# Table loads ahead, dots two steps later, half of the score sums on GpSimd: four edits to the indexer stage of a hybrid attention layer

## The chip, the cores and the metric

The kernel runs on one core of one Trainium2 chip. The time is device microseconds of one launch, the median of three runs: 1025.65 us (1023.9 to 1025.77). Five engines work side by side, each through its own instructions in the order of the program: PE (TensorE: matmuls into PSUM), DVE (VectorE), ACT (ScalarE), POOL (GpSimd, which also issues some DMAs) and SP (SyncE, which issues most DMAs). An instruction that waits for another engine holds up everything behind it on its own engine.

## What is computed

One layer: a projection of 272 tokens (16 meta tokens and 256 of the sequence), sparse attention beside a pooling mixer, a norm, and a gated feed-forward part. The change touches the indexer, which says which keys each query may see. Cut to what matters (T is 272, 16 indexer heads of width 64, top 64 of the keys):

```python
p = h @ W_in            # q | c_kv | q_idx | k_idx | w_idx | u
c_kv = rms_norm(c_kv, kv_norm_g)
dots  = einsum('bqhd,bsd->bqhs', q_idx * 64**-0.5, k_idx)
score = einsum('bqhs,bqh->bqs', relu(dots), w_idx * 16**-0.5)
score = where(causal, score, NEG_INF)
_, sel = top_k(score, 64)
bias = rel_bias[t5_bucket(max(dist, 0))]     # one table of 32 buckets x 8 heads
logits = q_abs . c_kv[sel] * 128**-0.5 + bias
p = softmax(logits); out = p . c_kv[sel]
```

After that come the values, the pooling, W_o, two layer norms and the feed-forward part, which hold most of the time and are not touched.

## The kernel before

**Number format.** Nearly every float32 matrix is split into an upper and a lower part of a narrower format: ACT copies (the upper part), DVE subtracts (the lower part). For weights this is `split_part`, L193 on ACT and L194 on DVE. A product is then two or three matmuls for each of its 16 K steps of 128 rows. In the indexer's projections (`paired`) a step is two matmuls: L316 with 416 columns (upper weights with both parts of x) and L317 with 208 (lower weights with the upper part of x).

**Weight stream.** `stream` lists the weight tiles in order: tiles 0 to 7 are the indexer's query projections (w_proj), 8 and 9 are w_uk and w_uv, then the other w_proj tiles and all the rest. Each is 1 MB: a DMA on SP (L199) into one of three `wraw` buffers, then split by L193 and L194 in two halves of 1024 (tile 10 in pieces of 512 and 1536) into one of three `whl` buffers. `weights()` calls for the tile two ahead of the one used. The next load into a `wraw` buffer waits until L194 is through with the tile in it.

**Start.** x comes with the first weights (L334), ACT and DVE split both (L339 to L342), and PE projects the indexer's key, its head weights and the latent c_kv (L388). From PSUM ACT and DVE make `kidx` (L395, L397), `wt` (L400), `kt` (L415) and the squares (L418). PE turns `wt` (L423), DVE copies it to `widx` (L424), the 16 head weights of each query.

**Indexer stage.** The loop L489 runs over j = 0 to 7; iteration j projects the queries of heads 2j and 2j + 1 (a pair). At its end ACT takes one half of the sum from PSUM (L502, `whole`), DVE adds the other (L503), and both write the pair's query in two parts, `qi` (L506 on ACT, L508 on DVE). The dots of pair j - 1 stand within iteration j: `dots` for the first head after nine K steps, for the second after twelve. A head has four matmuls (L477, L478: 144 keys for the first block of queries, 272 for the second); ACT applies the relu into `rl` (L480 for the first block, L481 for the second); DVE adds it, times the head's weight, to `score` (L483, for each block). The latent norm hangs on the same loop: PE sums the squares (L363) after j = 0, DVE transposes (L368) and scales (L432), POOL takes the power -0.5 (L433), DVE spreads it (L372) and scales the latent (L439), ACT and DVE split it (L441, L442).

`relative_bias()` is called after j = 1: it loads the table of biases (`rb_sb`, L454) and the one-hot buckets (`oh`, L456), multiplies them (L458), writes the product behind a stretch of NEG into `strip` (L460, L461), sends it to DRAM (L463, a DMA on POOL) and reads it back as Toeplitz blocks (L468, three DMAs on POOL).

**Keys.** The loop L518 makes eight heads of keys from w_uk (L522 to L524, copied by L526 on ACT); the dots of the last pair stand after head h = 2, and after heads 1 and 3 w_uv is split. Then come the values (L554 to L559), the top-k on DVE (L575, L576), which masks the bias (L580), and the query projections. The bias is first used by L622.

**What sets the order.** The program is written as one list; a scheduler then orders each engine's instructions by their place in that list and by when it reckons that each may run, and gives out the buffers of a tag. Tiles of tag t (`temp`, four buffers: `wt`, `sq`, `r`, `rb`, `rl`, `whole`, `strip` and, before, the two tables) and of tag w (`window`, three buffers, used by the pooling later on) are such.

## Time and profile before

| what | value |
|---|---|
| median of three runs | 1025.65 us |
| the profiled execution, its own time | 1026.09 us |
| its span, first to last instruction | 1024.3 us |
| mean granted clock of TensorE | 0.994 |

The span by stages, from the windows of the trace (us; busy time of each engine):

| stretch | what runs | length | PE | DVE | ACT | POOL | clock |
|---|---|---|---|---|---|---|---|
| 0 to 24 | start | 24.00 | 22.03 | 15.34 | 16.55 | 3.55 | 1.00 |
| 24 to 49.8 | indexer, j = 0 to 2 | 25.80 | 21.43 | 19.42 | 14.12 | 7.74 | 0.87 |
| 49.8 to 83.4 | indexer, j = 3 to 7 | 33.60 | 30.34 | 25.46 | 21.20 | 0.03 | 1.00 |
| 83.4 to 98.7 | keys, last dots, values | 15.30 | 14.59 | 12.88 | 11.96 | 0.30 | 1.00 |
| 98.7 to 143.3 | queries, top-k | 44.60 | 44.60 | 29.96 | 19.24 | 0.00 | 1.00 |
| 143.3 to 968 | attention, pooling, W_o, feed-forward | 824.70 | 824.70 | 749.66 | 502.98 | 167.42 | 1.00 |
| 968 to 1024.3 | last part and norm | 56.30 | 50.77 | 39.54 | 36.31 | 11.64 | 0.94 |

How to read it: busy time is the time in which an engine ran an instruction, waits left out. A wait in the trace's lists stands as "engine line <- whom it waited for". In a row of the timeline the first two numbers are start and length in us, then engine, line, operation, what is written and read, shape, and in brackets the idle time before it and what ended it. In a row of the windows the stretch and its length come first, then busy time and instructions of PE, PE's weight load, DVE, ACT and POOL, then the granted clock, the share of the DMA engines and GB/s.

### The profile page before, as it was taken

The numbers are of one execution on the slowest core, as the hardware profiler recorded it, in microseconds if no ns is written. First come the engines' busy times: TensorE is split into PE (matmuls) and PEld (weight loads), VectorE is DVE, ScalarE is ACT, GpSimd is POOL, SyncE is SP. The second block draws the span as 40 slices with busy tenths as digits, with TensorE's granted clock in tenths as the row PEclk, the third lists the DMA queues.
The fourth block names the chain that finished last, engine by engine and source line by source line (L and its number), as shares of the span: only waits on it lengthen the run. The fifth ranks groups of instructions, "written<-read, shape, count | busy, mean of one in ns | idle before, by whom it ended". The sixth has DMA issues, their size and how long they took to land.

```text
span 1024.3 us, 18956 instructions
## 1 busy us (share of the span) xinstructions
PE 1008.5 (98%) x7516; PEld 958.8 (94%) x7516; DVE 892.2 (87%) x1409; ACT 622.4 (61%) x1008; POOL 190.7 (19%) x246
## 2 busy tenths in 40 slices
PE   9899999999999999999999999999999999999997
PEld 8788999999999999999999999999999999999986
DVE  6788768767879998899999999999999999999876
ACT  7567446655457765666556665666656666566674
POOL 1300004324430032203121021210212102120031
PEclk9899999999999999999999999999999999999998
DMA  9656543454653569999888888888888889888584
GB/s 330 224 194 228 192 154 130 145 170 164 207 202 134 196 190 264 284 367 304 274 282 288 297 281 272 281 290 291 284 274 286 285 292 283 273 284 288 209 250 131
DMA packets 59753, 250.26 MB, mean 244 GB/s; under 512 B 21734, under 2 KB 22416, under 8 KB 32656
## 3 DMA queue, kind: packets, MB, share of 16 engines
q1 hardware_dynamic: 34592, 230.42, 62.6%
q0 software_dynamic: 7888, 16.14, 8.3%
q10 hardware_dynamic: 17184, 2.49, 1.5%
q8 instruction: 59, 0.97, 0.4%
q14 instruction: 30, 0.25, 0.1%
HBM read 232.50 MB, written 2.11 MB: 229 GB/s over the span
## 4 chain that ended last, share of the span: by engine, by line
PE 90%; DVE 3%; DMA 3%; issue 2%; ACT 1%; POOL 1%; SPq 0%; POOLq 0%; ACTq 0%; DVEq 0%
PE mm L308 66%; PE at L920 6%; PE at L919 6%; PE at L921 6%; DVE whl L194 1%; PE mm L316 1%; ACT whl L193 1%; DMA wraw<-in_w_proj 1%; PE mm L317 1%; DMA wraw<-in_w_down 1%; DMA oh<-in_onehot 1%; DMA wraw<-in_w_first 1%; PE at L477 0%; PE mm L620 0%; PE at L478 0%
## 5 line engine op out<-in xcount | busy, mean ns | idle before, releaser
L308 PEld LDWEIGHTS mm<-hp,whl 128*128 128x128 f32 x3840 | 456.9, 188 | 6.3
L308 PE MATMUL mm<-hp,whl 128*128 128x258 f32 x3840 | 458.9, 279 | 0.0
L194 DVE TENSOR_TENSOR whl<-wraw,whl 128x1024 fp32r<-128x1024 f32 (+2 forms) x312 | 370.6, 1215 | 34.3 <-ACT whl L193 33.3
L193 ACT ACTIVATE whl<-wraw 128x1024 fp32r<-128x1024 f32 (+2 forms) x312 | 304.1, 1021 | 72.4 <-PE mm L308 23.5
L194 DVE TENSOR_TENSOR whl<-room,whl 128x512 fp32r<-128x512 f32 (+1 forms) x104 | 118.0, 1164 | 1.9 <-ACT whl L193 1.6
L193 ACT ACTIVATE whl<-room 128x512 fp32r<-128x512 f32 (+1 forms) x104 | 98.4, 993 | 14.9 <-DVE room L205 7.5
L308 PE MATMUL mm<-xp,whl 128*128 128x258 f32 (+4 forms) x768 | 98.8, 285 | 0.0
L308 PEld LDWEIGHTS mm<-xp,whl 128*128 128x128 f32 x768 | 93.8, 188 | 0.9
L850 ACT ACTIVATE z<-mm,cv 128x256 f32<-128x256 f32 x40 | 22.6, 564 | 89.3 <-PE mm L308 89.3
L892 POOL TENSOR_TENSOR forms<-za 128x128 f32<-128x128 f32 x20 | 20.3, 1016 | 295.2 <-DVE za L868 230.4
L850 ACT ACTIVATE za<-mm,cv 128x256 f32<-128x256 f32 x40 | 22.6, 564 | 84.9 <-PE mm L308 83.6
L920 PE MATMUL at<-whl,gp 128*128 128x512 f32 x180 | 70.6, 393 | 0.0
L921 PE MATMUL at<-whl,gp 128*128 128x512 f32 x180 | 70.4, 392 | 0.0
L919 PE MATMUL at<-whl,gp 128*128 128x512 f32 x180 | 68.7, 392 | 0.0
L895 POOL TENSOR_TENSOR forms<-za 128x128 f32<-128x128 f32 x20 | 22.5, 1124 | 196.7 <-DVE za L868 144.0
L308 PE MATMUL mm<-mixp,whl 128*128 128x258 f32 x384 | 48.0, 280 | 0.0
L308 PE MATMUL mm<-mixa,whl 128*128 128x258 f32 x384 | 47.1, 278 | 0.0
L308 PEld LDWEIGHTS mm<-mixp,whl 128*128 128x128 f32 x384 | 46.1, 188 | 0.1
L308 PE MATMUL mm<-fold,whl 128*128 128x260 f32 x384 | 45.8, 280 | 0.0
L308 PEld LDWEIGHTS mm<-mixa,whl 128*128 128x128 f32 x384 | 45.6, 188 | 0.0
L308 PEld LDWEIGHTS mm<-fold,whl 128*128 128x128 f32 x384 | 45.5, 188 | 0.1
L316 PE MATMUL mm<-xp,whl 128*128 128x416 f32 x128 | 41.7, 381 | 0.0
(342 smaller groups left out, 1470.4 us busy)
## 6 DMA issues: line engine op xcount, KB each, us to landing
wraw<-in_w_up SPq DMA_DIRECT2D x62, 1024.0 KB, 5.1
wraw<-in_w_down SPq DMA_DIRECT2D x54, 1024.0 KB, 6.7
room<-in_w_up SPq DMA_DIRECT2D x26, 1024.0 KB, 5.2
room<-in_w_down SPq DMA_DIRECT2D x26, 1024.0 KB, 6.5
wraw<-in_w_proj SPq DMA_DIRECT2D x24, 1024.0 KB, 5.0
wraw<-in_w_o SPq DMA_DIRECT2D x16, 1024.0 KB, 4.9
y<-v POOLq DMA_DIRECT2D x27, 256.0 KB, 8.4
y<-u POOLq DMA_DIRECT2D x18, 256.0 KB, 4.8
```

What stands on the lines that cost most here:

```text
L193: upper = nc.scalar.activation(hl[:, 0, c], raw[:, c], AF.Copy)
L194: lower = nc.vector.tensor_tensor(hl[:, 1, c], raw[:, c], hl[:, 0, c].bitcast(F32), op=ALU.subtract)
L308: nc.tensor.matmul(ps, a, b, start=n == 0 and i == 0, stop=i == 2 and n == KT - 1)
L316: nc.tensor.matmul(ps[:, :2 * m], hl[:, 0, w], act[k].both(lo, hi), start=n == 0, stop=False)
L317: nc.tensor.matmul(ps[:, m:2 * m], hl[:, 1, w], act[k][:, 0, lo:hi], start=False, stop=n == KT - 1)
L850: nc.scalar.activation(z, src[:, 2:NQ], AF.Identity, bias=col(C_B, j), scale=col(C_W, 3 * j + 2))
L892: nc.gpsimd.tensor_tensor(s[:, 0], a21, a22, op=ALU.add)
L895: nc.gpsimd.tensor_tensor(s[:, 3], a11, a21, op=ALU.subtract)
L919: nc.tensor.matmul(ps, a[:, 0, i], hl[:, 0, w], start=j == 0, stop=False)
L920: nc.tensor.matmul(ps, a[:, 0, i], hl[:, 1, w], start=False, stop=False)
L921: nc.tensor.matmul(ps, a[:, 1, i], hl[:, 0, w], start=False, stop=j == n - 1)
```

## The change

Four edits, all around the indexer stage:

- `rb_sb` and `oh` get tiles of tag w, and their loads are issued where the bias tiles are made, ahead of the stage. `whole` moves from tag t to tag w.
- The dots of a pair stand after 11 and 14 K steps, where they stood after 9 and 12.
- The score sum of the first block, one DVE instruction, becomes two on POOL: rl times the head's weight, in place, and score plus that.
- The dots of the last pair stand after key head 4, where they stood after head 2.

```diff
--- before.py
+++ after.py
@@ -449,11 +449,12 @@
 
         return bias[:, h, ::-1]
 
+    rb_sb = window("rb_sb")[:32, :H]
+    nc.sync.dma_start(rb_sb, rel_bias)
+    oh = window("oh")[:32, :T]
+    nc.sync.dma_start(oh, onehot)
+
     def relative_bias():
-        rb_sb = temp([32, H], "rb_sb")
-        nc.sync.dma_start(rb_sb, rel_bias)
-        oh = temp([32, T], "oh")
-        nc.sync.dma_start(oh, onehot)
         ps = small()
         nc.tensor.matmul(ps[:H, :T], rb_sb, oh, start=True, stop=True)
         strip = temp([H, STRIP], "strip")
@@ -479,9 +480,10 @@
             rl = temp([P, KW], "rl")
             nc.scalar.activation(rl[:, :KA], pa_[:, S * i:S * i + KA], AF.Relu)
             nc.scalar.activation(rl[:, KA:], pb[:, :T], AF.Relu)
-            for i2, (a, b) in enumerate(((0, KA), (KA, KW))):
-                nc.vector.scalar_tensor_tensor(score[:, a:b], rl[:, a:b], widx[:, i2, h:h + 1], score[:, a:b],
-                                               op0=ALU.mult, op1=ALU.add)
+            nc.vector.scalar_tensor_tensor(score[:, KA:], rl[:, KA:], widx[:, 1, h:h + 1], score[:, KA:], op0=ALU.mult,
+                                           op1=ALU.add)
+            nc.gpsimd.tensor_tensor(rl[:, :KA], rl[:, :KA], widx[:, 0, h:h + 1].to_broadcast([P, KA]), op=ALU.mult)
+            nc.gpsimd.tensor_tensor(score[:, :KA], score[:, :KA], rl[:, :KA], op=ALU.add)
 
     queries = sb.tile([P, 2, 2, S], F32R, name="qi", tag="y", padded_shape=[P, 2, 2, KT * T // 4])
     nc.gpsimd.memset(queries[:, :, :, :ALL].bitcast(F32), 0.0)
@@ -489,16 +491,16 @@
     for j in range(8):
         hl = weights()
         ps = big()
-        paired(ps, hl, x_parts, TOPK, T, K_PROJ, k1=9)
+        paired(ps, hl, x_parts, TOPK, T, K_PROJ, k1=11)
         if j:
             pa_ = small()
             dots(j - 1, qis[j - 1], pa_, (0,))
-        paired(ps, hl, x_parts, TOPK, T, K_PROJ, k0=9, k1=12)
+        paired(ps, hl, x_parts, TOPK, T, K_PROJ, k0=11, k1=14)
         if j:
             dots(j - 1, qis[j - 1], pa_, (1,))
-        paired(ps, hl, x_parts, TOPK, T, K_PROJ, k0=12)
+        paired(ps, hl, x_parts, TOPK, T, K_PROJ, k0=14)
         qi = queries[:, j % 2]
-        whole = temp([P, NI], "whole")
+        whole = window("whole")[:, :NI]
         nc.scalar.activation(whole, ps[:, NI:2 * NI], AF.Copy)
         nc.vector.tensor_tensor(whole, ps[:, :NI], whole, op=ALU.add)
         for i in range(2):
@@ -524,7 +526,7 @@
             nc.tensor.matmul(ps[:, :T], uk[:, 1, w], ctp[:, c, 0, :], start=False, stop=c == 1)
         with tc.issue_after(query):
             key = nc.scalar.activation(kt[:, h, :], ps[:, :T], AF.Copy)
-        if h == 2:
+        if h == 4:
             dots(7, qis[7], big(), (0, 1), big)
         if h in (1, 3):
```

The line numbers of the changed kernel run up to two higher in this stage (L477 is L478 there, L483 stays for the second block, L485 and L486 are the sums on POOL, L458 is L459, L502 is L504, L508 is L510).

Where instructions stand, in three places. First SP, at the start of the weight stream; `wraw` with a number is a buffer's tile. Before:

```order
L199 DMA wraw_387<-in_w_proj 128x2048
L199 DMA wraw_394<-in_w_proj 128x2048
L199 DMA wraw_401<-in_w_proj 128x2048
L199 DMA wraw_455<-in_w_proj 128x2048
L199 DMA wraw_545<-in_w_proj 128x2048
L199 DMA wraw_613<-in_w_proj 128x2048
L199 DMA wraw_681<-in_w_proj 128x2048
L454 DMA rb_sb_531<-in_rel_bias 32x8
L456 DMA oh_533<-in_onehot 32x272
L199 DMA wraw_749<-in_w_proj 128x2048
```

The changed kernel, from the same place:

```order
L453 DMA rb_sb_385<-in_rel_bias 32x8
L455 DMA oh_387<-in_onehot 32x272
L199 DMA wraw_391<-in_w_proj 128x2048
L199 DMA wraw_398<-in_w_proj 128x2048
L199 DMA wraw_405<-in_w_proj 128x2048
L199 DMA wraw_459<-in_w_proj 128x2048
L199 DMA wraw_547<-in_w_proj 128x2048
L199 DMA wraw_617<-in_w_proj 128x2048
L199 DMA wraw_687<-in_w_proj 128x2048
L199 DMA wraw_757<-in_w_proj 128x2048
```

The two small loads, which stood behind seven w_proj loads, now stand ahead of the first. The rows of x's load and of the later weights keep their places.

Second ACT, from the last instruction of the start to the end of iteration j = 0; `whl_388` is tile 0, 395 tile 1, 402 tile 2, 456 tile 3. Before:

```order
L340 ACTIVATE whl_169<-wraw_l_186 128x336
L193 ACTIVATE whl_388<-wraw_387 128x1024 x2
L395 ACTIVATE kidx_351<-mm_204 64x272 x2
L415 ACTIVATE kt_367<-mm_205 128x272
L415 ACTIVATE kt_367<-mm_206 128x272
L193 ACTIVATE whl_395<-wraw_394 128x1024 x2
L418 ACTIVATE sq_369<-mm_205 128x272
L418 ACTIVATE sq_373<-mm_206 128x272
L193 ACTIVATE whl_402<-wraw_401 128x1024 x2
L502 ACTIVATE whole_441<-mm_408 128x208
L193 ACTIVATE whl_456<-wraw_455 128x1024
L506 ACTIVATE qi_385<-whole_441 64x208 x2
```

The changed kernel, whose tiles 0 to 3 are 392, 399, 406 and 460:

```order
L340 ACTIVATE whl_169<-wraw_l_186 128x336
L193 ACTIVATE whl_392<-wraw_391 128x1024
L395 ACTIVATE kidx_351<-mm_204 64x272 x2
L415 ACTIVATE kt_367<-mm_205 128x272
L415 ACTIVATE kt_367<-mm_206 128x272
L193 ACTIVATE whl_392<-wraw_391 128x1024
L418 ACTIVATE sq_369<-mm_205 128x272
L418 ACTIVATE sq_373<-mm_206 128x272
L193 ACTIVATE whl_399<-wraw_398 128x1024 x2
L193 ACTIVATE whl_406<-wraw_405 128x1024 x2
L504 ACTIVATE whole_445<-mm_412 128x208
L193 ACTIVATE whl_460<-wraw_459 128x1024
```

The second half of tile 0 stood ahead of `kidx` and `kt` and now stands behind them. DVE has the same move: its L194 for that half stood ahead of L397 and L400 and now stands behind both, and both halves of tiles 1 and 2 follow it ahead of `whole`.

Third DVE in iterations j = 1 and 2, from the scaling of the latent norm (L432) to the second pair's query; `whl` is tile 3 first, then tile 4. Before:

```order
L432 TENSOR_SCALAR rms_v_382<-r_448 128x9
L194 TENSOR_TENSOR whl_456<-wraw_455,whl_456 128x1024
L483 SCALAR_TENSOR_TENSOR score_359<-rl_487,widx_376,score_359 128x144
L483 SCALAR_TENSOR_TENSOR score_359<-rl_487,widx_376,score_359 128x272
L483 SCALAR_TENSOR_TENSOR score_359<-rl_503,widx_376,score_359 128x144
L483 SCALAR_TENSOR_TENSOR score_359<-rl_503,widx_376,score_359 128x272
L372 STREAM_TRANSPOSE rb_523<-rms_v_382 128x288
L503 TENSOR_TENSOR whole_516<-mm_462,whole_516 128x208
L439 SCALAR_TENSOR_TENSOR kt_367<-kt_367,cv_193,rb_523 128x272 x2
L194 TENSOR_TENSOR whl_546<-wraw_545,whl_546 128x1024
L508 TENSOR_TENSOR qi_385<-whole_516,qi_385 64x208 x2
```

The changed kernel:

```order
L432 TENSOR_SCALAR rms_v_382<-r_452 128x9
L194 TENSOR_TENSOR whl_460<-wraw_459,whl_460 128x1024
L483 SCALAR_TENSOR_TENSOR score_359<-rl_495,widx_376,score_359 128x272
L372 STREAM_TRANSPOSE rb_529<-rms_v_382 128x288
L461 MEMSET strip_539 8x400
L483 SCALAR_TENSOR_TENSOR score_359<-rl_512,widx_376,score_359 128x272
L439 SCALAR_TENSOR_TENSOR kt_367<-kt_367,cv_193,rb_529 128x272 x2
L505 TENSOR_TENSOR whole_522<-mm_466,whole_522 128x208
L462 COPY strip_539<-at_537 8x272
L194 TENSOR_TENSOR whl_548<-wraw_547,whl_548 128x1024
L510 TENSOR_TENSOR qi_389<-whole_522,qi_389 64x208 x2
```

The two sums of 128x144 are gone; the memset of `strip` and its copy from PSUM (L461 and L462, before L460 and L461) now stand ahead of tile 4's first half and of the second pair's query, and `whole` stands behind the two L439. On POOL the sums of the first two heads stand between the power L433 and the DMA of `strip`, and those of the next two behind the three DMAs that read it back. On PE the tables' matmul stands behind the last step of iteration j = 1, where it stood between two matmuls of the eighth step of j = 2, and `wt` is turned after three steps of j = 0, where it was after five.

## The prediction

> **What bounds the kernel now.** The first part of the page says which engine is full.

> ```profile
> PE 1008.5 (98%) x7516; PEld 958.8 (94%) x7516; DVE 892.2 (87%) x1409; ACT 622.4 (61%) x1008; POOL 190.7 (19%) x246
> ```

> PE is idle for 1024.3 - 1008.5 = 15.8 us in all, so a change that leaves its matmuls as they are can win little more than that, plus what a low clock costs. The waits of PE say whom it waits for.

> ```profile
> PE at L458 <- DMA oh<-in_onehot: 4.1, 1, 4.1
> PE at L477 <- DVE qi L508: 3.3, 5, 1.8
> ...
> PE mm L477 <- ACT rl L480: 0.7, 1, 0.7
> ```

> All three lie in the indexer stage (L489 to L531), and all three are touched. The windows put them in time: the wait of L458, the stretch after it, the iterations j = 3 to 6, and j = 7.

> ```profile
> 37.74:41.83 4.09, 0.00 (x1) 0.04 (x2) 3.97 (x7) 1.95 (x4) 1.70 (x2) 0.99 0.23 91
> 41.83:48.60 6.77, 6.77 (x24) 5.77 (x25) 1.61 (x5) 1.02 (x4) 2.10 (x4) 0.50 0.46 157
> 49.81:75.46 25.65, 24.23 (x161) 22.97 (x161) 20.20 (x36) 17.06 (x36) 0.02 (x1) 1.00 0.60 191
> 75.46:83.34 7.88, 6.04 (x42) 5.71 (x42) 5.25 (x9) 4.14 (x9) 0.00 (x0) 1.00 0.63 232
> ```

> The second row is the one to notice: after 4.09 us without a matmul the granted clock is 0.50 for 6.77 us. The wait costs its own length and half of the next stretch.

> **Part 1, the tables.** L456 waits on SP for a tile of tag t, and the load then runs behind a weight load.

> ```profile
> 11.39 0.43 SPq L348 DMA_DIRECT2D cv<-in_cols  x1
> 12.77 21.77 SPq L199 DMA_DIRECT2D wraw<-in_w_proj  x7
> 34.91 0.34 SPq L454 DMA_DIRECT2D rb_sb<-in_rel_bias  x1
> 35.80 0.32 SPq L456 DMA_DIRECT2D oh<-in_onehot  x1
> 35.80 5.89 DMA oh<-in_onehot
> ```

> Both loads now stand ahead of the first w_proj load. Two issues of 0.34 fit between the load of cv, whose issue ends at 11.82, and 12.77; the bytes (35 KB against 1024 KB for each weight tile) I take at nothing. Should they make that load late by a few tenths, ACT has them to spare: after the tile's first half (till 21.7) it now waits for PE until 22.94 (part 3). Gain: 4.09 + 6.77 / 2 = **7.5 us**.

> **Part 2, dots two steps later.** One iteration, j = 4, on ACT, DVE and PE:

> ```profile
> 56.26 0.34 ACT L502 ACTIVATE whole<-mm 128x208 f32<-128x208 f32 x1 [0.86 <-PE mm L317]
> 56.50 1.05 ACT L193 ACTIVATE whl<-wraw 128x1024 fp32r<-128x1024 f32 x1
> 57.59 1.23 DVE L194 TENSOR_TENSOR whl<-wraw,whl 128x1024 fp32r<-128x1024 f32 x1 [0.57 <-ACT whl L193]
> 58.84 0.77 DVE L508 TENSOR_TENSOR qi<-whole,qi 64x208 fp32r<-64x208 f32 x2
> 59.27 0.34 PE L477 MATMUL at<-kidx,qi 128*128 128x144 f32 x1 [0.36 <-DVE qi L508]
> ```

> The query of the last pair needs 59.27 - 56.2 = 3.07 us from the end of its projection. PE had done nine steps by 59.27 - 0.36 = 58.91, so a step takes 2.7 / 9 = 0.30. Eleven steps are 3.3: the wait of 0.36 goes, with 0.27 to spare. What is late next is nothing on PE: DVE and ACT are busy 20.20 and 17.06 of 25.65. Gain over four iterations: 25.65 - 24.23 = 1.4 of idle time, and for a PE that need not start anew 0.1 each by the first matmul (0.34 after the wait, 0.24 without one at 32.79 below), perhaps twice that with the step behind it; I take **2.0** (1.4 to 2.4). At j = 7 the tile is cut 512 + 1536 and the path is longer:

> ```profile
> 75.78 2.00 ACT L193 ACTIVATE whl<-wraw 128x512 fp32r<-128x512 f32 x2
> 77.82 1.76 DVE L194 TENSOR_TENSOR whl<-wraw,whl 128x1536 fp32r<-128x1536 f32 x1 [0.69 <-ACT whl L193]
> 80.03 0.34 PE L477 MATMUL at<-kidx,qi 128*128 128x144 f32 x1 [1.84 <-DVE qi L508]
> ```

> Here 1.84 becomes 1.84 - 0.6: gain **0.5**, with 0.1 off for part 4.

> **Part 3, what the scheduler moved.** The cover of the first tile's split goes. The rows of ACT and DVE before:

> ```profile
> 20.62 2.01 ACT L193 ACTIVATE whl<-wraw 128x1024 fp32r<-128x1024 f32 x2 [1.67 <-DMA wraw<-in_w_proj]
> 22.94 0.79 ACT L395 ACTIVATE kidx<-mm 64x272 fp32r<-64x272 f32 x2 [0.30 <-PE mm L388]
> 23.76 0.69 ACT L415 ACTIVATE kt<-mm 128x272 f32<-128x272 f32 x2
> 24.33 2.01 ACT L193 ACTIVATE whl<-wraw 128x1024 fp32r<-128x1024 f32 x2
> 21.72 2.36 DVE L194 TENSOR_TENSOR whl<-wraw,whl 128x1024 fp32r<-128x1024 f32 x2 [2.00 <-ACT whl L193]
> ```

> ```profile
> 24.11 6.52 SPq L199 DMA_DIRECT2D wraw<-in_w_proj  x3
> wraw<-in_w_proj SPq DMA_DIRECT2D x24, 1024.0 KB, 5.0
> 32.79 0.24 PE L477 MATMUL at<-kidx,qi 128*128 128x144 f32 x1
> 33.14 2.73 POOL L433 TENSOR_TENSOR rms_v<-rms_v,half 128x9 f32<-128x9 f32 x1 [29.02 <-DVE rms_v L432]
> ```

> Tile 0's second half was split by 24.08 and freed the buffer into which tile 3 was loaded at 24.11. Now its L193 stands behind kidx and kt, which wait for PE until 22.94: it starts at 24.33, its L194 ends at 24.33 + 1.06 + 1.22 = 26.6, tile 3 lands at 26.6 + 5.0 = 31.6. On ACT and DVE tile 3's first half stands ahead of the first pair's query: 31.6 + 1.06 + 1.22 + 0.37 = 34.3. PE asks for it at 32.79 + 0.6 = 33.4. A **new wait of 0.9**, with 0.2 for the new start: -1.1 (0 to -1.6).

> It goes on. L432 follows the query (35.0), L433 takes 2.73 on POOL (37.8 instead of 35.87), and DVE then does in order the transpose, the memset of strip, a score sum, two L439, whole, the copy of strip, L194 and the query. The table of DVE in this stage has most of the durations:

> ```profile
> L194 DVE TENSOR_TENSOR whl<-wraw,whl 128x1024 fp32r<-128x1024 f32 x19 | 22.9, 1216 | 4.0 <-ACT whl L193 3.7
> L483 DVE SCALAR_TENSOR_TENSOR score<-rl,widx,score 128x272 f32<-128x272 f32 x16 | 8.0, 500 | 0.6 <-ACT rl L481 0.6
> L508 DVE TENSOR_TENSOR qi<-whole,qi 64x208 fp32r<-64x208 f32 x16 | 5.9, 370 | 0.9 <-ACT qi L506 0.4
> L483 DVE SCALAR_TENSOR_TENSOR score<-rl,widx,score 128x144 f32<-128x144 f32 x16 | 5.9, 366 | 5.0 <-ACT rl L480 4.9
> ```

> With 0.4 to 0.5 for each of the six smaller ones not listed that makes some 4.3 us: 42.1. PE, back at 34.3, needs 2.8 for the rest of the iteration, 0.5 for the tables' matmul and 3.3 for eleven steps: 40.9. A **second new wait of 1.2**, which part 4 lengthens.

> **Part 4, sums on GpSimd.** DVE loses 16 sums of 0.37 on 128x144; POOL gets 32 operations of that width, a form not in the trace. Nearest rows, alone and beside DVE:

> ```profile
> 153.20 0.64 POOL L681 TENSOR_TENSOR win<-u 128x273 f32<-128x273 f32 x1 [63.33 <-ACT u L677]
> 153.92 3.89 POOL L681 TENSOR_TENSOR win<-win 128x271 f32<-128x271 f32 x3
> 154.03 3.18 DVE L194 TENSOR_TENSOR whl<-wraw,whl 128x1024 fp32r<-128x1024 f32 x2 [0.71 <-ACT whl L193]
> ```

> Three POOL additions take 1.3 each where one alone takes 0.64, and two L194 take 3.18, not about 2.35: 0.83 for two POOL operations between them, 0.41 each. For 144 columns a hold lies between 0.22 (by width) and 0.41, and I take 0.3; a POOL operation between 0.34 and 1.3. Per pair POOL needs 1.4 to 5.2 of some 5.9, so it keeps up. It stands idle otherwise, apart from the strip's DMAs, which now wait behind the first two heads and hold up the next two; four rl buffers cover that. In the second new wait four POOL operations meet DVE's path, of which two delay it: -0.6. From there to the end of the stage I put -0.2. The second wait is then 1.8 with 0.2 for the start: **-2.0** (-0.5 to -2.8).

> [...]

> Late sums delay the top-k, not PE:

> ```profile
> L580 DVE SCALAR_TENSOR_TENSOR bias<-work,bias x8: 579/582/584, 109.4 to 112.9; 128x416 f32<-128x416 f32 x8
> L622 DVE SCALAR_TENSOR_TENSOR lg<-mm,bias x8: 572/577/591, 145.0 to 197.8; 128x416 f32<-128x416 f32 x8
> ```

> The masked bias is ready some 31 us before its first use.

> **Part 5, last dots two heads later.** Their wait of 0.7 is for L480 behind an L193 on ACT. Two heads later a second L193 (1.05) and two more copies stand ahead of it, against two heads of matmuls on PE: between 0.7 won and 0.5 lost, I take -0.2. x's load on SP moves with them, some 1.5 us, and one weight load behind it; both are wanted many microseconds later.

> **Sum.** 7.5 + 2.0 + 0.5 - 1.1 - 2.0 - 0.2 - 0.2 = 6.5 off the profiled execution's 1026.09 (span 1024.3 and 1.8 around it): 1019.6. The median of the runs, 1025.65, lies 0.44 below that execution, so I forecast **1019.2 us**.

> **Rivals.** (a) *The start hides it*: ACT or the load is sooner than I reckon and neither new wait shows. For it: at 32.79 no wait is listed. Against: both engines work in order. 7.5 + 2.0 + 0.5 - 0.4 = 9.6, so 1016.1. (b) *DVE and POOL exclude each other in each iteration*: one or two holds of 0.3 to 0.4 fall between L194 and the query and use up the 0.27 to spare. Part 2 falls from 2.0 to about 0.4 and part 4 costs another 0.6: 6.5 - 2.2 = 4.3, so 1021.3. Against it: ACT has the last rl of a pair ready before whole (0.86 idle ahead of it, 0.6 of which the later dots take), and the L194 on the path starts 1.3 after whole, time for two operations of 0.34 to 0.64. [...] (c) *Slower: POOL becomes the bound.* If an operation with the broadcast weight is dear, a pair costs 4p on POOL, and through the four rl buffers PE follows. From p = 1.5 POOL is slower than PE; from about 1.9 the gain is gone. At L433's 2.73 the last pair could start only at 38 + 6 x 10.9 = 103, not some 2 us after 83.34: 17 to 18 later, 1043. Against it: 0.64 for twice the width. (d) *No change*: a new wait grows to the 4 us of the old one and the clock halves again: 6.5 - 3.4 - 2 = 1.1, so 1024.6. Against: 1.84 at j = 7 left the clock at 1.00.

> **Chances.** Forecast 0.55, (a) 0.17, (b) 0.17, (c) 0.04, (d) 0.07. The ends of the unknown costs in parts 2 to 5 give 1016 to 1022, and (a) and (b) lie inside: range 1016.0 to 1022.5. A measurement tells about 0.2%, 2 us, from no change. Faster 0.89, the same 0.07, slower 0.04.

> **What would show it.** L459 with no wait and the clock at 1.00 through the stage; waits of PE on the query of about 1 us at the first pair and 2 at the second, none at the next four, some 1.2 at the last; w_proj's fourth load issued near 26.6; an iteration of 5.9 us instead of 6.41. Wrong would be: a listed wait on GpSimd by ACT's rl, iterations above 6.2, or a clock row of 0.50 before the last slice.

## The result, and the profile after

| | runs | median us | lowest to highest |
|---|---|---|---|
| before | 4 | 1025.22 | 1023.90 to 1025.77 |
| changed | 4 | 1018.89 | 1018.50 to 1019.12 |
| before, beside a second series | 11 | 1025.41 | 1023.35 to 1028.01 |
| changed, second series | 6 | 1019.93 | 1018.55 to 1021.59 |

The ratio is 0.994 (95% interval 0.9923 to 0.9957) in the first series and 0.9942 (0.9926 to 0.9958) in the second. Of 1025.2 that is 6.0 to 6.2 us, and the two intervals together reach from 4.3 to 7.9. The forecast was 1019.2 with a range of 1016.0 to 1022.5. The profiled execution of the changed kernel took 1019.05, with a span of 1017.3. Its first part on the page:

```profile
PE 1005.9 (99%) x7516; PEld 956.1 (94%) x7516; DVE 889.9 (87%) x1393; ACT 622.0 (61%) x1008; POOL 211.2 (21%) x278
```

PE is now idle for 11.4 us instead of 15.8. With the same 7516 instructions it is also busy 2.6 us less: the stretch of 6.77 at half clock, which is gone, had held some 3.4 of extra busy time (half of it), and elsewhere PE is busy 0.8 longer. The waits of PE in the changed kernel (us in total, times, longest):

```profile
PE at L478 <- DVE qi L510: 2.8, 3, 1.3
...
PE mm L478 <- ACT rl L481: 0.7, 1, 0.7
PE mm L317 <- DVE whl L194: 0.7, 1, 0.7
...
PE at L423 <- DVE wt L400: 0.3, 1, 0.3
```

The wait of 4.1 us on the table is gone, and of five waits on a query three are left. They are these, in PE's timeline (start, duration, and in brackets the idle time ahead):

```profile
34.36 0.33 PE L478 MATMUL at<-kidx,qi 128*128 128x144 f32 x1 [0.33 <-DVE qi L510]
...
42.44 0.34 PE L478 MATMUL at<-kidx,qi 128*128 128x144 f32 x1 [1.29 <-DVE qi L510]
...
73.25 0.33 PE L478 MATMUL at<-kidx,qi 128*128 128x144 f32 x1 [1.17 <-DVE qi L510]
```

PE waits at the first pair, at the second and at the last, and at none of the four between. The windows of the changed kernel, cut where PE begins j = 0, 1 and 2, then j = 3 to 6 and j = 7 (length, then the busy time of PE, PEld, DVE, ACT and POOL, then the granted clock):

```profile
22.98:30.32 7.34, 6.33 (x41) 5.57 (x39) 7.25 (x10) 6.71 (x11) 0.00 (x0) 1.00 0.54 194
30.32:37.55 7.23, 6.90 (x45) 5.89 (x43) 5.23 (x9) 4.51 (x10) 2.56 (x1) 1.00 0.87 314
37.55:44.99 7.44, 6.15 (x41) 5.79 (x41) 7.11 (x14) 4.46 (x10) 4.59 (x9) 1.00 0.32 131
45.16:68.73 23.57, 23.55 (x161) 22.96 (x161) 19.54 (x30) 17.00 (x36) 14.09 (x22) 1.00 0.75 254
68.73:75.96 7.23, 6.06 (x42) 5.74 (x42) 4.59 (x8) 4.10 (x9) 2.18 (x5) 1.00 0.65 224
```

The first three of these in the kernel before, from its own trace:

```profile
23.50:29.85 6.35, 6.07 (x40) 5.57 (x39) 6.18 (x9) 5.85 (x11) 0.00 (x0) 1.00 0.69 210
29.85:35.84 5.99, 5.99 (x42) 5.89 (x41) 5.75 (x12) 3.75 (x8) 2.70 (x1) 1.00 0.92 346
35.84:49.64 13.80, 9.71 (x45) 8.43 (x43) 7.99 (x16) 5.00 (x11) 4.88 (x7) 0.75 0.46 154
```

So the stage changed by +0.99 (j = 0), +1.24 (j = 1, which now holds the tables' matmul), -6.36 (j = 2), -2.08 (j = 3 to 6, 25.65 before) and -0.65 (j = 7, 7.88 before): -6.9 in these two executions. The start of j = 0 differs by another -0.5, which no edit accounts for: PE waits 1.2 us for the split of x (L388) in one and 0.4 in the other, and 0.2 in the second profile of before. From the end of the stage to the end of the span nothing is won: 941.0 us before, 941.3 after.

### The profile page after: what moved, and what is told of

It is laid out like the page before. It is cut to its first block, busy times and chain, and to the rows that moved or that the text cites. A ratio compares the mean times of both kernels' runs of the same rounds, so it can differ in the third digit from the quotient of the medians.

```text
span 1017.3 us, 18967 instructions
## 1 busy us (share of the span) xinstructions
PE 1005.9 (99%) x7516; PEld 956.1 (94%) x7516; DVE 889.9 (87%) x1393; ACT 622.0 (61%) x1008; POOL 211.2 (21%) x278
## 4 chain that ended last, share of the span: by engine, by line
PE 90%; DMA 3%; DVE 2%; issue 2%; POOL 1%; ACT 1%; SPq 0%; POOLq 0%; ACTq 0%; DVEq 0%
PE mm L308 66%; PE at L922 6%; PE at L921 6%; PE at L923 6%; PE mm L316 1%; DMA wraw<-in_w_proj 1%; DVE whl L194 1%; DMA wraw<-in_w_down 1%; PE mm L317 1%; DMA wraw<-in_w_first 1%; ACT whl L193 1%; POOL gb L1044 0%; PE mm L622 0%; PE at L478 0%; PE at L657 0%
## 5 line engine op out<-in xcount | busy, mean ns | idle before, releaser
L194 DVE TENSOR_TENSOR whl<-wraw,whl 128x1024 fp32r<-128x1024 f32 (+2 forms) x312 | 371.6, 1218 | 37.3 <-ACT whl L193 36.3
L193 ACT ACTIVATE whl<-wraw 128x1024 fp32r<-128x1024 f32 (+2 forms) x312 | 304.1, 1021 | 76.7 <-PE mm L308 23.6
L194 DVE TENSOR_TENSOR whl<-room,whl 128x512 fp32r<-128x512 f32 (+1 forms) x104 | 118.1, 1165 | 2.0 <-ACT whl L193 1.8
L193 ACT ACTIVATE whl<-room 128x512 fp32r<-128x512 f32 (+1 forms) x104 | 98.4, 993 | 15.2 <-DVE room L205 7.5
L894 POOL TENSOR_TENSOR forms<-za 128x128 f32<-128x128 f32 x20 | 20.3, 1016 | 296.2 <-DVE za L870 231.5
L897 POOL TENSOR_TENSOR forms<-za 128x128 f32<-128x128 f32 x20 | 22.5, 1124 | 195.5 <-DVE za L870 142.9
L923 PEld LDWEIGHTS at<-whl,gp 128*128 128x128 f32 x180 | 33.9, 188 | 7.2
## 6 DMA issues: line engine op xcount, KB each, us to landing
wraw<-in_w_up SPq DMA_DIRECT2D x62, 1024.0 KB, 5.2
wraw<-in_w_down SPq DMA_DIRECT2D x54, 1024.0 KB, 6.6
room<-in_w_up SPq DMA_DIRECT2D x26, 1024.0 KB, 5.2
room<-in_w_down SPq DMA_DIRECT2D x26, 1024.0 KB, 6.6
wraw<-in_w_proj SPq DMA_DIRECT2D x24, 1024.0 KB, 5.0
wraw<-in_w_o SPq DMA_DIRECT2D x16, 1024.0 KB, 4.8
```

The source lines that it names most:

```text
L193: upper = nc.scalar.activation(hl[:, 0, c], raw[:, c], AF.Copy)
L194: lower = nc.vector.tensor_tensor(hl[:, 1, c], raw[:, c], hl[:, 0, c].bitcast(F32), op=ALU.subtract)
L894: nc.gpsimd.tensor_tensor(s[:, 0], a21, a22, op=ALU.add)
L897: nc.gpsimd.tensor_tensor(s[:, 3], a11, a21, op=ALU.subtract)
L923: nc.tensor.matmul(ps, a[:, 1, i], hl[:, 0, w], start=False, stop=j == n - 1)
```

## Experiments

They were run in three series, each beside the kernel before on one chip, and the ratio is to that kernel in the same series (its medians were 1025.69 for e1 to e6, 1025.41 for after_again to e8, and 1026.46 for the last four). The last row shows what such a ratio is worth: the kernel before, compared with itself in this way, came out at 0.9988, so 0.1% between two rows is not read as an effect.

| run | runs | median us | ratio, 95% interval |
|---|---|---|---|
| e1_tables: tables alone | 12 | 1026.26 | 0.9996 (0.9985 to 1.0008) |
| e2_dots: later dots alone | 12 | 1021.26 | 0.9964 (0.9948 to 0.9980) |
| e3_pool: sums on GpSimd alone | 12 | 1027.26 | 1.0012 (1.0000 to 1.0023) |
| e6_warm: before, wait filled | 12 | 1025.26 | 0.9997 (0.9984 to 1.0011) |
| after_again: changed | 6 | 1019.93 | 0.9942 (0.9926 to 0.9958) |
| e5_nopool: changed, sums on DVE | 6 | 1019.55 | 0.9940 (0.9924 to 0.9955) |
| e7_tabq: changed, tables on GpSimd's queue | 6 | 1019.10 | 0.9930 (0.9913 to 0.9948) |
| e8_tabq_nopool: both | 6 | 1018.49 | 0.9928 (0.9911 to 0.9945) |
| e10_tables_warm: tables alone, waits filled | 7 | 1023.40 | 0.9969 (0.9957 to 0.9981) |
| e9_allpool: changed, all sums on GpSimd | 10 | 1030.17 | 1.0035 (1.0024 to 1.0047) |
| e11_later: as e8, dots later still | 5 | 1018.38 | 0.9914 (0.9898 to 0.9929) |
| before_again: before | 11 | 1025.31 | 0.9988 (0.9977 to 0.9999) |

**One part alone.** The first three runs each carry one edit of the diff and leave the rest of the kernel as before.

> The kernel before with the tables edit alone (both tables loaded ahead into tiles of their own). Theory T (the edit removes the wait of 4.1 us and the half clock behind it, and its two small loads and the new order of tile 0 bring the start waits of the changed kernel): the half-clock stretch and the wait go, -7.5; a wait of some 0.66 on tile 0's split near 23.3, some 0.9 at the first pair (0.33 in the changed kernel, and the dots stand two steps of 0.3 earlier), some 1.5 at the second, 0.2 for new starts: about -4.2, so 1021.0 us (1020.2 to 1022). Rival R1 (the start waits come from the sums on GpSimd): no new waits at the start, -7.5, so 1017.7. The waits at j = 3 to 6 (0.36 each) and 1.84 at j = 7 stay in either.

The tables alone gained nothing that can be measured. Theory T had asked for -4.2, R1 for -7.5, and both fell. The trace of this run has the wait on the table gone, and its windows show what came in its place:

```profile
41.36:44.77 3.41, 1.47 (x11) 1.21 (x10) 3.32 (x7) 2.84 (x6) 1.25 (x4) 1.00 0.08 28
44.77:48.18 3.41, 3.41 (x15) 3.33 (x14) 2.20 (x5) 0.90 (x3) 2.38 (x3) 0.50 0.44 115
75.49:78.90 3.41, 1.64 (x12) 1.36 (x11) 2.67 (x4) 1.56 (x3) 0.00 (x0) 1.00 0.32 135
78.90:82.31 3.41, 3.41 (x15) 3.36 (x15) 1.13 (x4) 0.98 (x3) 0.00 (x0) 0.50 0.87 303
```

PE idles 1.94 of a stretch of 3.41 at the second pair and 1.77 of one at the last, and behind each the clock is 0.50 for just 3.41. That costs 1.7 us each (half of 3.41), so here a wait much shorter than 4.1 halves the clock as well. The two, with a second wait of 1.94 where T had 1.5, make up the 3.8 us that T is short.

> The kernel before with the later dots alone. Theory T: the four waits of 0.36 at j = 3 to 6 go and 1.84 at j = 7 becomes some 1.2; the wait of 4.1 us on the table and the clock of 0.50 behind it stay: -2.5, so 1022.7 us (1022.2 to 1023.5). Rival R2 (DVE or ACT is the pace of an iteration, so that the wait only moves to the next projection): iterations stay at 6.4 us, 1024.6 to 1025.2.

Faster by 3.7 us (2.0 to 5.3), more than the forecast but within the interval. R2 fell: no query waits but the last, and the wait of L458 is shorter than before and left the clock alone:

```profile
PE at L458 <- DMA oh<-in_onehot: 2.5, 1, 2.5
...
PE at L477 <- DVE qi L508: 1.2, 1, 1.2
```

> The kernel before with the first block's sums on GpSimd alone. Theory T: the sums are not on the path in j = 3 to 6 and their holds lengthen single DVE operations: L439 from 0.49 to some 0.7, an L194 to 1.4; +0.3 (0 to +1.0), so 1025.5 (1025.2 to 1026.2), with the query waits of PE the same or longer. Rival R3 (time freed on DVE brings the query sooner): each of the five query waits shorter by 0.2 to 0.37, -0.8 to -1.5, so 1023.7 to 1024.4.

Slower by 1.2 us (0 to 2.4): R3 fell. T's sign agrees, but the difference is no larger than that of the kernel before from itself, so a cost is not shown. This run's profile, too, has a wait of 2.6 on the table with the clock at 1.00 behind it, and 1.86 us of idle time ahead of the last pair with the clock at 0.50 behind it.

The three ratios add up to -2.9 us (by their intervals give or take some 2), half of what the kernel with all edits gains. What is missing had to be found.

**The wait filled.** In the kernel before, ahead of the tables' matmul:

```diff
         ps = small()
+        for _ in range(16):
+            nc.tensor.matmul(ps[:H, :P], ident[:, :H], ct[:, 1, :P], start=True, stop=True)
         nc.tensor.matmul(ps[:H, :T], rb_sb, oh, start=True, stop=True)
```

> The kernel before with 16 matmuls of 128x128 f32 on PE ahead of the tables' matmul, whose results nothing reads: they fill the wait of 4.1 us in part, and nothing else is changed (the tables' matmul comes 2 steps sooner). Theory T (4.1 us without a matmul is what halves the clock): the longest idle stretch falls below 2 us, the granted clock of the stretch behind it is 1.00 and not 0.50, -3.4 less 0.3 to 0.6 for the two steps that now stand behind the wait: -2.9, so 1022.3 us (1021.9 to 1022.9). Rival R4 (the half clock has another cause, or ACT and DVE bound that stretch, so that a faster PE gains nothing there): within 0.7 us of before, 1024.5 to 1025.9.

The clock did as T said. From the tables' matmul to the start of j = 3, in this run and then in the kernel before:

```profile
43.67:49.01 5.34, 5.34 (x36) 4.85 (x36) 2.37 (x6) 1.38 (x4) 1.03 (x2) 1.00 0.58 199
```

```profile
41.83:49.64 7.81, 7.81 (x32) 6.80 (x32) 2.21 (x6) 1.38 (x4) 3.14 (x5) 0.57 0.47 144
```

That is 2.5 us less with two steps more in it. But the ratio is 0.9997, -0.3 us (-1.6 to 1.1), so T's -2.9 was missed in the time. In the profiled execution the load of `oh` was issued at 37.78, where it was at 35.80 before, and the tables' matmul began at 43.67 instead of 41.83, so that j = 3 begins only 0.6 us sooner (49.01 against 49.64). For the others the next run bears on why: the wait is not so long in each execution. The sixteen useless matmuls take 3.66 us, more than a wait of 2.3 to 2.6 and the two steps of 0.3 together, so there they can cost what they win. That is an argument from these numbers and was not tried with fewer of them.

**The kernel before, profiled again.**

> The kernel before once more, for a second profile. Theory T3 (the wait on the table's load varies by execution, with the landing of the weight load issued just ahead of it, and the half clock follows only where 1.7 us of a stretch of 3.41 are idle): the wait lies between 2.5 and 4.1 us, with 0, one or two stretches at half clock behind it; the median stays 1025.5 us. Rival R10 (both are fixed): 4.1 us, and the clock at 0.50 for 6.8 us behind it.

```profile
PE at L477 <- DVE qi L508: 3.2, 5, 1.8
PE at L458 <- DMA oh<-in_onehot: 2.3, 1, 2.3
```

```profile
37.44:40.85 3.41, 1.13 (x6) 0.44 (x5) 3.30 (x8) 2.54 (x6) 0.41 (x2) 1.00 0.42 169
40.85:44.26 3.41, 3.41 (x14) 3.33 (x14) 2.04 (x4) 0.51 (x2) 2.15 (x2) 0.50 0.34 65
74.98:78.39 3.41, 1.57 (x12) 1.40 (x11) 2.83 (x5) 1.02 (x4) 0.00 (x0) 1.00 0.23 43
78.39:81.80 3.41, 3.41 (x15) 3.34 (x14) 1.18 (x3) 0.69 (x2) 0.00 (x0) 0.50 0.66 269
```

The same code with the same span (1024.2 against 1024.3): the wait is 2.28 and not 4.09, the half clock behind it lasts 3.41 and not 6.77, and a second stretch of 3.41 at half clock stands behind the wait of 1.84 at j = 7, which had left the clock alone in the first profile. R10 falls. T3 holds in that the wait and the half clock vary, though 2.28 lies below its lower bound of 2.5: the four profiles with this wait (the other two are of e2_dots and e3_pool) have 4.1, 2.3, 2.5 and 2.6.

**The clock held up in the tables edit.** As e1_tables, and ahead of the dots of two pairs:

```diff
             pa_ = small()
+            for _ in range({2: 5, 7: 4}.get(j, 0)):
+                nc.tensor.matmul(pa_[:, :P], ident, wholes[j - 1][:, :P], start=True, stop=True)
             dots(j - 1, qis[j - 1], pa_, (0,))
```

> The tables edit alone, as in e1_tables, and ahead of the dots of the second and of the last pair five and four matmuls of 128x128 f32 on PE, whose results nothing reads: they stand in the waits of 1.94 and 1.77 us and are shorter than these. Theory T2 (the two waits halve the clock behind them, and that is why the tables edit alone gained nothing): no clock of 0.50 before the last slice, the two stretches of 3.41 us at half clock go, -3.4 in an execution that had both: 1022.4 us (1021.6 to 1023.4). Rival R9 (the tables edit gains nothing for another reason, such as its start waits): as e1_tables, 1025.3 to 1026.5.

The nine useless matmuls make the kernel faster: -3.2 us (1.9 to 4.4) against before, where e1_tables had -0.4. Against before_again, which ran in the same series, it is some 2 us (0.9969 to 0.9988). T2 holds, at the slow end of its range (1023.40 of 1021.6 to 1023.4), and R9 falls. The stretches that hold the two waits, and those behind them:

```profile
41.63:45.04 3.41, 2.82 (x21) 2.38 (x20) 3.32 (x6) 2.84 (x6) 1.25 (x4) 1.00 0.02 4
45.04:48.45 3.41, 3.41 (x25) 3.37 (x24) 2.30 (x6) 1.85 (x5) 2.18 (x3) 1.00 0.56 133
75.70:79.11 3.41, 2.54 (x20) 2.34 (x19) 2.60 (x5) 0.65 (x3) 0.00 (x0) 1.00 0.39 86
79.11:82.52 3.41, 3.41 (x28) 3.40 (x27) 1.96 (x5) 2.13 (x7) 0.00 (x0) 1.00 0.52 221
```

PE still waits for the same queries, but idles 0.59 and 0.87 of a stretch, and the clock stays at 1.00.

**The changed kernel with one part undone.** The plain kernel ran beside them:

> The changed kernel once more, beside kernels that undo one part of it. Theory T2 (a clock of 0.50 follows a stretch of 3.41 us of which PE idles some 1.7 or more; the tables edit alone leaves two such waits, of 1.94 and 1.77, the later dots bring both below 1.3, so the two edits pay together what neither pays alone): 0.994 of the time before, 1019.3 us (1018.4 to 1020.2), no wait above 1.5 before the last slice and no clock of 0.50 there. Rival R6 (the edits add up: 0 for the tables, -4 for the dots, +1.2 for the sums, as their runs alone gave): -2.8, so 1022.6 us.

T2 holds. In this second profile the waits on the queries are 0.59, 1.29 and 1.17, and no clock of 0.50 stands ahead of the last slice. R6, a plain sum of the parts, fell: all six times are below its 1022.6, though that sum is itself uncertain by some 2 us, so the traces carry more of this verdict than the times.

In e5_nopool the two GpSimd lines of the score sum go and DVE has both blocks again, as before:

> The changed kernel with all score sums back on DVE. Theory T2 (GpSimd's sums hold DVE up and win nothing on PE's path): the wait at the second pair falls from 1.29 to some 0.6, the one at j = 7 from 1.17 by some 0.1, 0.5 to 1.2 faster than the changed kernel: 1018.4 us. Rival R7 (DVE's work on the sums would stand ahead of the query): waits at j = 3 to 6 of 0.1 to 0.3 appear, 0.5 to 1.5 slower than the changed kernel: 1020.3 us.

No difference that can be measured; both fell as to size. Over j = 3 to 6 no wait appears. The wait at the second pair is 1.32, as long as with the sums on GpSimd, but that does not show that the holds (the time by which DVE's instructions are longer beside GpSimd's) are no part of it, since DVE's order ahead of this query changed too. Among its rows in e5_nopool, between the transpose and the query, are these:

```profile
38.16 0.74 DVE L484 SCALAR_TENSOR_TENSOR score<-rl,widx,score 128x144 f32<-128x144 f32 x2
38.82 0.91 DVE L439 SCALAR_TENSOR_TENSOR kt<-kt,cv,rb 128x272 f32<-128x272 f32 x2
39.93 0.43 DVE L442 TENSOR_TENSOR ctp<-kt,ctp 128x272 fp32r<-128x272 f32 x1
```

In the changed kernel L439 takes 1.31 there, but one sum of 128x272 (0.41) stands in place of the two of 128x144, and a copy of 0.42 in place of L442. What the holds win or cost at this place stays open. They can be seen elsewhere, and are small: the sum of 128x272 takes 0.59 us with GpSimd's sums beside it and 0.50 without, the split of a half tile 1.28 and 1.22. DVE's rows for the same stretch (44 to 76 us), in the changed kernel and then without the sums on GpSimd:

```profile
L194 DVE TENSOR_TENSOR whl<-wraw,whl 128x1024 fp32r<-128x1024 f32 x9 | 11.5, 1281 | 2.2 <-ACT whl L193 2.1
L483 DVE SCALAR_TENSOR_TENSOR score<-rl,widx,score 128x272 f32<-128x272 f32 x12 | 7.0, 587 | 3.3 <-ACT rl L482 3.1
```

```profile
L194 DVE TENSOR_TENSOR whl<-wraw,whl 128x1024 fp32r<-128x1024 f32 x9 | 11.0, 1223 | 2.0 <-ACT whl L193 1.7
L484 DVE SCALAR_TENSOR_TENSOR score<-rl,widx,score 128x272 f32<-128x272 f32 x12 | 6.0, 496 | 0.0
```

In e7_tabq both table loads are issued on another queue, and nothing else differs:

```diff
-    nc.sync.dma_start(rb_sb, rel_bias)
+    nc.gpsimd.dma_start(rb_sb, rel_bias)
-    nc.sync.dma_start(oh, onehot)
+    nc.gpsimd.dma_start(oh, onehot)
```

> The changed kernel with both table loads issued on GpSimd's queue, ahead as before: the same bytes at the same time, but SP is free, so that tile 0's second half stands ahead of kidx and kt again. Theory T2 (the order on ACT and DVE makes the start waits): tile 3's load is issued near 24.1 and not 26.4, no wait at the first pair (0.33 now) and none on tile 0's split (0.66 now), the second pair's wait shorter by some 0.3: 1.0 to 1.5 faster than the changed kernel, 1018.0 us. Rival R8 (the bytes of the tables ahead of the first weight load make them): tile 0 lands as late as in the changed kernel, near 21.5, and the wait of 0.66 stays: within 0.4 of the changed kernel, 1019.3 us.

The order came back: ACT splits the whole of tile 0 in one piece ahead of kidx, no wait stands at the first pair, and the second pair's is 0.61. Tile 3's load was issued at 25.86 and not near 24.1, as tile 0 itself landed late, at 22.3, in this execution, the slowest of the six. The median is 0.8 below the changed kernel's, and the intervals overlap, so a gain in time is not shown. How late tile 0 lands does not tell R8 apart: it landed between 20.5 and 22.5 us with and without the table loads ahead of it (20.5 and 20.8 in the two profiles of before, 21.5 and 20.8 in those of the changed kernel).

> The changed kernel with both: table loads on GpSimd's queue and all score sums on DVE. Theory T2: both gains, no wait of PE between 24 and 70 us above 0.5: 1.5 to 2.5 faster than the changed kernel, 1017.2 us. Rivals R7 and R8: 0 to 1.5 slower than the changed kernel, 1019.3 to 1020.8 us.

1.4 below the changed kernel by the medians, again inside the intervals. Its profile is of its slowest execution and says little for T2: tile 3's load took 7.5 us there, and the waits at the first two pairs were 0.86 and 1.33.

**A double dose of GpSimd.** In the changed kernel:

```diff
-            nc.vector.scalar_tensor_tensor(score[:, KA:], rl[:, KA:], widx[:, 1, h:h + 1], score[:, KA:], op0=ALU.mult,
-                                           op1=ALU.add)
-            nc.gpsimd.tensor_tensor(rl[:, :KA], rl[:, :KA], widx[:, 0, h:h + 1].to_broadcast([P, KA]), op=ALU.mult)
-            nc.gpsimd.tensor_tensor(score[:, :KA], score[:, :KA], rl[:, :KA], op=ALU.add)
+            for i2, (a, b) in enumerate(((0, KA), (KA, KW))):
+                nc.gpsimd.tensor_tensor(rl[:, a:b], rl[:, a:b], widx[:, i2, h:h + 1].to_broadcast([P, b - a]),
+                                        op=ALU.mult)
+                nc.gpsimd.tensor_tensor(score[:, a:b], score[:, a:b], rl[:, a:b], op=ALU.add)
```

> The changed kernel with all score sums on GpSimd, the second block's too: twice the suspected holds, and DVE without any sum. Theory T2 (POOL keeps up, each operation 0.4 to 1.4 us and four a pair on 144 and 272 columns, some 4 of the 5.8 us of an iteration; its holds cost a little): 0.4 to 1.2 slower than the changed kernel, 1020.7 us, iterations 5.8 to 6.1. Rival (c) of the prediction (POOL becomes the bound): iterations above 6.2, ACT's rl waits for POOL, 1023 or more. Rival R3 (time freed on DVE is worth more than the holds): 0.3 to 1.0 faster, 1019.2 us.

Rival (c) appears, at twice the dose, though at 1030 and not at its 1043, and T2 and R3 fall: some 10 us slower than the changed kernel. The window from j = 3 to the end of the stage, the waits there, and DVE's split from 44 to 76 us:

```profile
44.63:82.46 37.83, 31.55 (x202) 29.90 (x201) 23.33 (x26) 20.50 (x46) 32.09 (x42) 0.96 0.64 213
```

```profile
ACT rl L481 <- POOL score L485: 8.1, 4, 2.6
...
PE at L478 <- DVE qi L509: 5.8, 4, 2.1
```

```profile
L194 DVE TENSOR_TENSOR whl<-wraw,whl 128x1024 fp32r<-128x1024 f32 x10 | 15.1, 1522 | 2.1 <-ACT whl L193 2.0
```

POOL is busy 32.1 of 37.8, ACT's rl waits for it through the rl buffers, `whole` stands behind that rl on ACT, and PE behind the query. DVE does fewer instructions, and those that stay take longer: the split of a half tile 1.52 us, and 1.22 with no sums on GpSimd. The window is 7.0 longer than in the changed kernel (30.81), with a stretch at half clock in it, from 79.76, behind 2.04 of idle time. Most of the rest lies later: the top-k waits for the last sums until 96.22, where it began at 84.26 in the changed kernel, splits of weights stand behind it on DVE, and PE waits for one of them:

```profile
112.08 4.16 PE L308 MATMUL mm<-xp,whl 128*128 128x258 f32 x32 [2.77 <-DVE whl L194]
```

So "late sums delay the top-k, not PE" in the prediction holds for the changed kernel, and not at this dose.

**The dots later still.** As e8_tabq_nopool, with k1 = 13 and 15 in place of 11 and 14:

> As e8_tabq_nopool (table loads on GpSimd's queue, sums on DVE), with the dots another step or two later (after 13 and 15 steps of 16). Theory T2 (each step put ahead is 0.3 off a wait that is still there, and nothing where there is none): the wait at j = 7 from 1.17 to some 0.6, the second pair's from 1.33 to 0.7, none at j = 3 to 6: 1.0 to 1.6 faster than e8_tabq_nopool, 1017.2 us. Rival R2 (an iteration is set by DVE or ACT, and the wait moves elsewhere): within 0.4 of e8_tabq_nopool, 1018.5 us, or later for the last dots, which then follow the last projection by one step: 1019 us.

The waits went as T2 said, and R2's moved wait did not come: none at the first two pairs, and this at the last, with the last dots' own wait grown from 0.67:

```profile
PE mm L478 <- ACT rl L481: 0.9, 1, 0.9
...
PE at L478 <- DVE qi L509: 0.6, 1, 0.6
```

The time is another matter. Its ratio is the lowest of all, but the before of that series was slow, and its median, 1018.38, is that of e8. Divided by the 0.9988 of before_again, which ran beside it, its ratio is 0.9926, that of e8 (0.9928). So the waits are shorter and a gain in time is not shown.

## Why the prediction was right, and where it was not

The sum (6.5 off) and the measurement (6.0 to 6.2) agree. Most of the signs that the forecast named came as well: no wait of L459, the clock at 1.00 through the stage, tile 3's load issued at 26.44 for 26.6, iterations of 5.9. Step by step:

- **Part 1, 7.5: the mechanism holds, the size belongs to one execution.** The wait and the half clock did go, and in the two traces compared j = 2 is shorter by 6.36. But in the second profile of before the same two terms are 2.28 + 3.41 / 2 = 4.0. And the edit by itself gave -0.4 and not the -4.2 that the same reasoning asked of it, since the waits it leaves, of 1.94 and 1.77, keep halving the clock; with these filled it gave -3.2, or some 2 against before_again. A span is a sum of such draws, so the total of one profiled execution can stand near the median while a term in it does not.
- **Part 2, 2.0 and 0.5: right as waits.** 25.65 became 23.57, which is 2.08, and the last wait went from 1.84 to 1.17. What failed is the sentence under rival (d), "1.84 at j = 7 left the clock at 1.00". By the stretches of that trace (its half clock begins at 41.77, and eleven of 3.413 later is 79.3) the wait from 78.19 to 80.03 was cut into 1.12 and 0.72. In before_again, e1_tables and e3_pool it fell into one stretch (1.84, 1.77 and 1.86 us idle) and the clock of the next was 0.50, which costs 1.7, half of 3.41. The later dots remove this cost too, and bring the second pair's wait from 1.94 in e1_tables to 1.29. That is why the edits together pay about 3 us more than the single runs add up to, give or take 3 by the intervals: no wait long enough is left.
- **Part 3, -1.1 and -2.0: the new waits came where they were placed, and were smaller.** At the first pair 0.33 and 0.59 in the two profiles, not 0.9: the query was ready at 34.3 as reckoned, but PE came later, in the first profile by the 0.66 that it had waited for tile 0's split. That wait was not foreseen; it is absent from the second profile. At the second pair 1.29 both times, not 1.8. Of the 0.6 put on GpSimd's holds there, 0.4 is seen on L439 (1.31 for two, 0.91 before), but without the sums DVE's order differs and the wait is the same 1.32, so how much of it is due to the holds stays open.
- **Part 4: DVE's instructions take longer beside GpSimd's, a cost in time is not shown at this dose.** A GpSimd operation took 0.62 us on average, between the 0.34 and 1.3 of the bounds. The rows:

```profile
L486 POOL TENSOR_TENSOR score<-score,rl 128x144 f32<-128x144 f32 x16 | 10.0, 624 | 1.2
L485 POOL TENSOR_TENSOR rl<-rl,widx 128x144 f32<-128x144 f32 x16 | 9.9, 618 | 18.4 <-ACT rl L481 18.4
```

  Rival (b) did not come: an iteration is 23.57 / 4 = 5.9, without a wait of PE. One sign that the prediction counted as wrong did appear, a listed wait of ACT's rl on GpSimd, once in j = 4 and once in j = 5:

```profile
ACT rl L481 <- POOL rl L485: 1.5, 2, 0.8
```

  It cost nothing, as PE was busy for 23.55 of 23.57 over these iterations, so a wait of ACT alone was too strict a sign. That DVE and POOL exclude each other, as rival (b) has it, no run shows. What they show is longer instructions: DVE's sum of 128x272 takes 0.59 with these operations about and 0.50 without them (e5_nopool), and with twice as many (e9_allpool) the half tile's split goes from 1.28 to 1.52. What it costs in time here is not shown.
- **Part 5, -0.2: nothing to be seen.** The wait of the last dots is 0.67, and was 0.71, and behind the stage the two spans differ by 0.3. This edit was not run alone.

So the total was right for reasons that were half luck. The 4.09 and the 6.77 were larger than usual in the profiled execution, and the half clock at j = 7, which is there in other executions, was missing from it: two errors of opposite sign.

## What to carry to other kernels

Before a term is sized by a wait on a transfer, or by the slow clock behind a wait, look at a second execution: here the wait was 4.1 in one and 2.3 in another of the same code, at the same total time. In the indexer stage a wait of PE was worth its own length where it left at most 1.51 us of a stretch of 3.41 idle (e2_dots), and 1.7 us more, half of the 3.41 at a clock of 0.50 behind it, where it left 1.77 (e1_tables) or more. So edits that shorten waits are judged together. Where a wait can't be removed, useless matmuls in it can be worth their place if they are shorter than the wait: nine won 2 to 3 us here, and sixteen in another wait won nothing. Moving sums to an idle GpSimd cost nothing measurable with 16 of 32 and some 10 us with all of them.

## What the runs showed of the hardware

```profile
37.60:41.01 3.41, 1.90 (x13) 1.60 (x11) 3.38 (x8) 3.17 (x8) 0.51 (x2) 1.00 0.79 303
41.01:44.42 3.41, 2.40 (x15) 1.96 (x16) 3.12 (x7) 0.47 (x1) 1.50 (x1) 1.00 0.00 1
```

In before, behind a stretch that was wholly idle (38.36 to 41.77), the half clock lasted 6.83 us, two stretches. At the end of the kernel it stood behind less idle time in most profiles: 1.0 to 1.5 us in the stretch ahead (1.28 in before, 1.46 in the changed kernel); what differs there was not tried. Where the stretches begin differs from one execution to the next (half clock from 41.77 in before and from 40.85 in before_again), which may be a part of the spread of the times; no run shows how large a part.
